# A two-layer attention trunk: attention of one head woven, matmul by matmul, into the projections of the next

## The chip, the cores and the metric

The kernel runs on all eight cores of one Trainium2 chip, one batch element a core, and the cores do not talk to each other. The time is device microseconds of the slowest core, and a lower one is better. A kernel on all cores has two states here. Most executions are fast and agree within 0.3%. In others the cores of one die (0 to 3 or 4 to 7), or of both, show a lower granted clock of TensorE and the run takes some per cent longer.

TensorE is called PE below, as in the profile, with PEld for its weight loads. ScalarE is ACT, VectorE is DVE, GpSimd is POOL, and SP issues most of the transfers.

## The reference

Two layers, x of 2048 rows and 2048 columns on each core. Cut to what matters:

```python
def fox_mixer(h, w_in, b_f, w_out):                 # layer 0: 16 heads of 128
    q, k, v, z, f = split(h @ w_in)
    c = cumsum(log_sigmoid(f + b_f))                # a forget gate for each head
    for i in range(S // Q_BLOCK):                   # causal
        s = q_i @ k.T * scale + c_t - c_s
        s = where(mask, s, -inf)
        outs.append(softmax(s) @ v)
    return (concat(outs) * silu(z)) @ w_out

def diff_mixer(...):                                # layer 1: 8 heads, two 128-wide maps, values 256 wide
    ...
        s = q_i @ k.T * scale + bias                # T5 bias, a constant beyond 128 positions
        p = softmax(where(mask, s, -inf))
        a = p[:, :, 0] - lam * p[:, :, 1]
    ...                                             # RMSNorm of a head, gain
    return (o * silu(z)) @ w_out

for i in range(2):
    x = layer_norm(ALPHA * x + mixer_i(x), ln_g[i], ln_b[i])
```

## The kernel before

Each layer is eight units of 256 columns: two FoX heads, or one differential head. A unit first runs all its projections (q and k at L489, v and z at L517), and only then its attention. A tile of the attention is one block of 128 keys against up to 256 queries: a score matmul, an exponential on ACT, and one or two matmuls with the values. The tile loop keeps these three apart by one tile each.

```python
def do_unit(u, slots):
    proj_fm(sq, qT, r_qT, "act")                    # L489, 512 columns a matmul
    ...
    proj_fm(sk, kT, r_kT, "dve")
    ...
    proj_tm(sv, evac_v)                             # L517, 256 columns
    ...
    proj_tm(sz_slot, evac_z)                        # L547: ACT applies Silu
    ...
    def qk(t):                                      # bank = t % 3
        e.matmul(pb[bank][:, 0:w], lhsT=kT[...], rhs=qT[...], start=True, stop=(len(extra) == 0))
        for n, (k, rhs, _) in enumerate(extra):     # L601: causal mask or T5 bias, added by PE
            e.matmul(pb[bank][:, k * 128:(k + 1) * 128], lhsT=ident[:], rhs=rhs, start=False, ...)
    ...
    for t in range(T + 2):
        if t < T:
            qk(t)
        if 0 <= t - 1 < T:
            ex(t - 1)                               # L618 (FoX) or L623: exponential
        if t - 2 >= 0:
            pv(t - 2)                               # L632: values
```

After the eighth unit come the output projection (L764), the residual and LayerNorm, and the next layer.

The softmax here doesn't subtract the row's maximum and nothing guards it: scores larger than these inputs give would overflow.

Of the kernel before, what the change touches and what calls it, by code (L numbers as in the profile page):

```python
# [16 lines left out]
NB = 16  # L17
KC = 16
# [5 lines left out]
FOX_IN = 8208  # L24
NUM_BUCKETS = 32
MAX_DISTANCE = 128
BIG = 262144.0
EW = 383
# [7 lines left out]

class Prog:
    ENG = ("pe", "act", "dve", "pool", "sp")
# [8 lines left out]
    def _dep(self, op, other):  # L47
        if other is None or other is op:
            return
        if other.dkey is not None:  # L50
            op.waits.append(other)
            return
        if not other.sig:
            lst = self.q[other.eng]
            for k in range(other.idx + 1, len(lst)):
                if lst[k].sig and lst[k].dkey is None and lst[k] is not op:
                    other = lst[k]
                    break
            else:
                other.sig = True  # L60
        op.waits.append(other)

    def _access(self, op, reads, writes):
        for (rg, lo, hi) in reads:
            recs = self.regions.setdefault(rg, [])
            for r in recs:
                if r[0] < hi and lo < r[1]:
                    self._dep(op, r[2])
                    r[3][op.hkey] = op
        for (rg, lo, hi) in writes:  # L70
            recs = self.regions.setdefault(rg, [])
            new = []
            for r in recs:
# [16 lines left out]
    def op(self, eng, fn, reads=(), writes=(), sig=None):  # L90
        o = Op(eng, fn, eng)
        o.idx = len(self.q[eng])
        o.sig = (eng != "pe") if sig is None else sig
        self._access(o, reads, writes)
        self.q[eng].append(o)
        return o
# [20 lines left out]
    def emit(self):  # L117
# [9 lines left out]
        with nc.Block() as block:  # L127
            def mk(ename):
                def body(e):
                    seen = {}  # L130
                    for o in self.q[ename]:
                        for w in o.waits:
# [4 lines left out]
                            if seen.get(k, 0) < v:  # L137
                                e.wait_ge(s, v)  # L138
                                seen[k] = v
# [13 lines left out]

def _t5_bucket(n):
# [7 lines left out]
def _consts():  # L162
    c = np.zeros((128, 3 * 128 + EW), np.float32)
    c[:, 0:128] = np.eye(128, dtype=np.float32)
    c[:, 128:256] = np.triu(np.ones((128, 128), np.float32))
    c[:, 256:384] = 1.0
    for m in range(127, EW):
        c[_t5_bucket(m - 127), 384 + m] += 1.0
        c[31, 384 + m] -= 1.0
    return c  # L170

def build_program(layers):
    nc = bass.Bass("TRN2", target_bir_lowering=False)
    dram_in = lambda n, s: nc.dram_tensor(n, s, F32, kind="ExternalInput").ap()
    x_in = dram_in("x", [S, D])
    xs_in = dram_in("xs", [4, 128, KC * 512])
    consts = dram_in("consts", [128, 3 * 128 + EW])
    ln_g = dram_in("ln_g", [DEPTH, D])
    ln_b = dram_in("ln_b", [DEPTH, D])
    w_in = {}  # L180
    w_out = {}
    if 0 in layers:
        w_in[0] = dram_in("w_in0", [4, 8, 128, KC * 256])
        w_f = dram_in("w_f", [128, KC * 16])
        w_out[0] = dram_in("w_out0", [4, 128, KC * 512])
        b_f = dram_in("b_f", [1, 16])
    if 1 in layers:
        w_in[1] = dram_in("w_in1", [4, 8, 128, KC * 256])
        w_out[1] = dram_in("w_out1", [4, 128, KC * 512])
        lam_q = dram_in("lam_q", [1, 256])  # L190
        lam_k = dram_in("lam_k", [1, 256])
        subln_g = dram_in("subln_g", [1, 256])
        rel_bias = dram_in("rel_bias", [32, 8])
        escr = nc.dram_tensor("escr", [8, 128, EW], F32).ap()
    y_out = nc.dram_tensor("y", [S, D], F32, kind="ExternalOutput").ap()
    x1d = nc.dram_tensor("x1d", [S, D], F32).ap() if len(layers) > 1 else None

    with ExitStack() as st:
        P = Prog(nc, st)
        sb = lambda n, s, d: st.enter_context(nc.sbuf_tensor(n, s, d))  # L200
        XA = sb("XA", [128, 4, KC, 512], BF16)
        XB = sb("XB", [128, 4, KC, 512], BF16)

        def xs(buf, k0, k1, t0, t1):
            st_ = t0 // 512
            lo = t0 - st_ * 512
            hi = t1 - st_ * 512
            if k1 is None:
                return buf[:, st_, k0, lo:hi]
            return buf[:, st_, k0:k1, lo:hi]  # L210
        W = [sb("W%d" % i, [128, KC, 256], BF16) for i in range(3)]
        UW = 18432
        U = sb("U", [128, UW], BF16)
        LW = 7168
        L = sb("L", [128, LW], BF16)
        ident = sb("ident", [128, 128], BF16)
        tri_bf = sb("tri_bf", [128, 128], BF16)
        nmask_bf = sb("nmask_bf", [128, 128], BF16)
        tbt = sb("tbt", [32, 8], F32)
        gtok = [sb("gtok%d" % i, [128, 2, 256], BF16) for i in range(2)]  # L220
        rin = sb("rin", [128, 16], F32)
        lnst = sb("lnst", [128, 32], F32)
        pb = [st.enter_context(nc.psum_tensor("pb%d" % i, [128, 512], F32)) for i in range(8)]

        def rX(buf, kc0, kc1, t0, t1):
            st_ = t0 // 512
            lo, hi = t0 - st_ * 512, t1 - st_ * 512
            if lo == 0 and hi == 512:
                return [(buf, (st_ * KC + kc0) * 1024, (st_ * KC + kc1) * 1024)]
            return [(buf, ((st_ * KC + kc) * 512 + lo) * 2, ((st_ * KC + kc) * 512 + hi) * 2) for kc in range(kc0, kc1)]  # L230
        def rU(lo, hi):
            return [("U", lo * 2, hi * 2)]
        def rL(lo, hi):
            return [("L", lo * 2, hi * 2)]
        def rW(i):
            return [("W%d" % i, 0, KC * 256 * 2)]
        def rPB(i, lo=0, hi=2048):
            return [("pb%d" % i, 0, 2048)]
        def rS(name, lo=0, hi=1 << 20):
            return [(name, lo, hi)]  # L240

        qT = U[:, 0:4096].rearrange("p (m t) -> p m t", m=2)
        kT = U[:, 4096:8192].rearrange("p (m t) -> p m t", m=2)
        V4 = U[:, 8192:12320].rearrange("p (b m c) -> p b m c", b=16, m=2)
        V3 = U[:, 8192:12320].rearrange("p (b c) -> p b c", b=16)
        sz = U[:, 12320:16416].rearrange("p (b c) -> p b c", b=16)
        PT_OFF = 16416
        Pt = [U[:, PT_OFF + s * 256: PT_OFF + (s + 1) * 256] for s in range(4)]
        def r_qT(m, t0, t1): return rU(m * 2048 + t0, m * 2048 + t1)
        def r_kT(m, t0, t1): return rU(4096 + m * 2048 + t0, 4096 + m * 2048 + t1)  # L250
        def r_V(b0, b1): return rU(8192 + b0 * 258, 8192 + b1 * 258)
        def r_sz(b0, b1): return rU(12320 + b0 * 256, 12320 + b1 * 256)
# [28 lines left out]
        def make_layer(li, Xbuf, Xname, Gbuf, Gname, resid_src, resid_reg, out_dst, out_reg, make_next):  # L281
# [218 lines left out]
            def do_unit(u, slots):  # L500
# [223 lines left out]
                for t in range(T + 2):  # L724
                    if t < T:
                        qk(t)
# [224 lines left out]
```

## Time and profile before

| | before |
|---|---|
| time, two fast runs of three | 3348.43 and 3349.73 us (the third, 3596.69, is slow) |
| matmuls, and the sum of their columns | 23,274, 6.905 million |
| the same at N / 2.4 + 2.5 ns each | 2935 us |
| distances between matmul starts beyond that, summed over the trace | 361.4 us |
| ACT table loads | 33 |

The last row but one is worked out from the trace. From the start of each matmul to the start of the next, N / 2.4 + 2.5 ns are taken off, where N is the number of columns; what remains is a gap of PE. With 28 us before the first matmul and 12 after the last the four amounts give some 3336 of 3347.6 us.

The prediction shows the stages. The next lines are the two kinds of unit as a whole, as busy time by stretch (columns: from and to in us, length, then busy us and instruction count of PE, PEld, DVE, ACT and POOL, then granted clock, DMA share and GB/s).

```profile
280.39:453.55 173.16, 164.48 (x1250) 106.08 (x1249) 31.22 (x98) 68.59 (x162) 2.11 (x4) 0.99 0.14 25
1920.07:2097.01 176.94, 171.98 (x1343) 118.84 (x1341) 58.70 (x184) 61.99 (x162) 9.59 (x20) 1.00 0.13 25
```

Over a whole unit ACT has only 68.59 of 173 us, or 61.99 of 177, of work. There is room to hide all of it, if it is spread over the unit and not pressed into the attention.

### The profile page before, as it was taken

How to read it: one execution, taken by the hardware profiler on the slowest of the kernel's cores; microseconds unless marked ns; L12 is line 12 of the kernel's file. 1: busy time of each engine (PE TensorE's matmuls, PEld its weight loads, DVE VectorE, ACT ScalarE, POOL GpSimd, SP SyncE). 2: the span in 40 equal slices, each digit the busy share in tenths (PEclk: the TensorE clock that was granted, in tenths of full speed). 3: DMA queues.
4: the chain of work that ended last, by engine and by line, in shares of the span. 5: the costliest groups of instructions: out<-in, count | busy, mean ns of one | idle time of the engine just before them, and what ended most of it. 6: DMA issues, size and time to landing. Idle time of an engine off the chain costs nothing.

```text
span 3347.6 us, 64426 instructions; the slowest of 8 cores (3340.9 to 3347.6 us)
## 1 busy us (share of the span) xinstructions
PE 3177.2 (95%) x23284; PEld 2027.3 (61%) x23284; DVE 998.7 (30%) x2802; ACT 1173.2 (35%) x2764; POOL 105.5 (3%) x220
## 2 busy tenths in 40 slices
PE   6899898989898999999999999999999999999998
PEld 2747475656566565644457575757676766767443
DVE  0121212121212121246523323242415151514555
ACT  0160707070707061633314233241506060606211
POOL 1000000000000000000000000000000000000000
PEclk9999999999999999999999999999999999999999
DMA  8202020202011110744311010202020202006343
GB/s 141 45 11 39 14 39 14 39 14 38 14 26 26 26 27 14 130 149 146 151 51 27 18 34 14 39 14 39 3 38 14 39 14 39 14 14 102 135 155 139
DMA packets 26754, 171.03 MB, mean 51 GB/s; under 512 B 3376, under 2 KB 7248, under 8 KB 8272
## 3 DMA queue, kind: packets, MB, share of 16 engines
q0 software_dynamic: 12240, 92.41, 15.6%
q1 hardware_dynamic: 14208, 74.51, 6.1%
q8 instruction: 196, 3.21, 0.4%
q14 instruction: 110, 0.90, 0.1%
HBM read 224.19 MB, written 35.12 MB: 77 GB/s over the span
## 4 chain that ended last, share of the span: by engine, by line
PE 85%; ACT 6%; issue 4%; DVE 2%; DMA 2%; ACTq 0%; POOL 0%; DVEq 0%; SPq 0%; POOLq 0%
PE pb L517 27%; PE pb L489 26%; PE pb L764 13%; PE pb L632 12%; ACT U L618 5%; PE pb L598 5%; PE pb L601 2%; DMA XA<-xs 1%; PE pb L644 1%; DMA U<-x 0%; PE pb L807 0%; DVE rin L667 0%; ACTq L138 0%; ACT L618 0%; ACT U L623 0%
## 5 line engine op out<-in xcount | busy, mean ns | idle before, releaser
L632 PE MATMUL pb<-U 128*128 128x129 bf16 (+1 forms) x4352 | 725.1, 247 | 109.0 <-ACT U L618 40.1
L598 PE MATMUL pb<-U 128*128 128x256 bf16 (+1 forms) x2304 | 603.3, 269 | 0.0
L632 PEld LDWEIGHTS pb<-U 128*128 128x128 bf16 x4352 | 323.2, 97 | 399.5 <-issue 332.8
L489 PE MATMUL pb<-XA,W 128*128 128x512 bf16 x2048 | 448.9, 382 | 29.9 <-DMA XA<-xs 29.9
L618 ACT ACTIVATE U<-pb,L 128x256 bf16<-128x256 f32 (+1 forms) x1152 | 451.3, 460 | 24.4 <-PE pb L598 10.6
L517 PE MATMUL pb<-W,XA 128*128 128x256 bf16 x4096 | 450.5, 273 | 0.0
L517 PE MATMUL pb<-W,XB 128*128 128x256 bf16 x4096 | 449.6, 273 | 0.0
L489 PE MATMUL pb<-XB,W 128*128 128x512 bf16 x2048 | 444.6, 379 | 1.3 <-ACT XB L816 1.3
L623 ACT ACTIVATE U<-pb 128x256 bf16<-128x256 f32 (+1 forms) x1152 | 400.4, 372 | 105.6 <-PE pb L598 38.5
L517 PEld LDWEIGHTS pb<-W,XA 128*128 128x128 bf16 x4096 | 401.9, 98 | 49.2 <-issue 0.3
L517 PEld LDWEIGHTS pb<-W,XB 128*128 128x128 bf16 x4096 | 400.5, 98 | 47.9
L489 PEld LDWEIGHTS pb<-XA,W 128*128 128x128 bf16 x2048 | 200.7, 98 | 271.8 <-issue 36.6
L489 PEld LDWEIGHTS pb<-XB,W 128*128 128x128 bf16 x2048 | 199.5, 98 | 239.5 <-issue 1.4
L547 ACT ACT_TABLE_LOAD x16 | 20.5, 1283 | 916.1 <-PE pb L517 916.1
L496 DVE CAST U<-pb 128x512 bf16<-128x512 f32 x128 | 88.6, 692 | 772.2 <-PE pb L489 563.3
L598 PEld LDWEIGHTS pb<-U 128*128 128x128 bf16 x2304 | 224.6, 97 | 11.9
L764 PE MATMUL pb<-XA,XB 128*128 128x512 bf16 x1024 | 225.4, 381 | 2.2 <-DVE U L769 2.2
L764 PE MATMUL pb<-XB,XA 128*128 128x512 bf16 x1024 | 223.0, 381 | 0.0
L494 ACT ACTIVATE U<-pb 128x512 bf16<-128x512 f32 x128 | 76.2, 597 | 394.6 <-PE pb L489 394.6
L540 DVE CAST U<-pb 128x512 bf16<-128x512 f32 x128 | 88.7, 693 | 356.2 <-PE pb L517 356.2
L547 ACT ACTIVATE U<-pb 128x512 bf16<-128x512 f32 x128 | 76.4, 597 | 304.5 <-PE pb L517 304.3
L764 PEld LDWEIGHTS pb<-XA,XB 128*128 128x128 bf16 x1024 | 99.6, 98 | 124.9 <-issue 8.9
(87 smaller groups left out, 1709.5 us busy)
## 6 DMA issues: line engine op xcount, KB each, us to landing
W<-w_in POOLq DMA_DIRECT2D x62, 1024.0 KB, 8.9
U<-x SPq DMA_DIRECT2D x16, 1024.0 KB, 5.0
x1d<-U SPq DMA_DIRECT2D x16, 1024.0 KB, 3.9
U<-x1d SPq DMA_DIRECT2D x16, 1024.0 KB, 4.9
y<-U SPq DMA_DIRECT2D x16, 1024.0 KB, 4.3
XA<-w_out POOLq DMA_DIRECT2D x4, 2048.0 KB, 25.8
XB<-w_out POOLq DMA_DIRECT2D x4, 2048.0 KB, 25.0
XA<-xs POOLq DMA_DIRECT2D x2, 2048.0 KB, 56.5
```

The costliest lines, as they stand in the source:

```text
L489: ins = e.matmul(pb[bk][:, :], lhsT=W[slot][:, kc, m * 128:(m + 1) * 128], rhs=Xbuf[:, tc, kc, :], start=(kc == 0), stop=(kc == KC - 1))
L494: fn = lambda e, m=m, tc=tc, bk=bk: e.activation(out=dstT[:, m, tc * 512:(tc + 1) * 512], in_=pb[bk][:, :], func=AF.Copy)
L496: fn = lambda e, m=m, tc=tc, bk=bk: e.tensor_copy(out=dstT[:, m, tc * 512:(tc + 1) * 512], in_=pb[bk][:, :])
L517: ins = e.matmul(pb[bk][:, bb * 256:(bb + 1) * 256], lhsT=xs(Xbuf, kc, None, b * 128, (b + 1) * 128), rhs=W[slot][:, kc, :], start=(kc == ...
L540: P.op("dve", lambda e: e.tensor_copy(out=dst, in_=src), reads=rPB(bk), writes=r_V(2 * bp, 2 * bp + 2))
L547: P.op("act", lambda e: e.activation(out=sz[:, 2 * bp:2 * bp + 2, :], in_=src, func=AF.Silu), reads=rPB(bk), writes=r_sz(2 * bp, 2 * bp + 2))
L598: ins = e.matmul(pb[bank][:, 0:w], lhsT=kT[:, m, j * 128:(j + 1) * 128], rhs=qT[:, m, q0:q0 + w], start=True, stop=(len(extra) == 0))
L601: ins = e.matmul(pb[bank][:, k * 128:(k + 1) * 128], lhsT=ident[:], rhs=rhs, start=False, stop=(n == len(extra) - 1))
L618: P.op("act", lambda e: e.activation(out=Pt[s][:, 0:w], in_=src, func=AF.Exp, bias=bsel[:, m, j, 2 * I:2 * I + 1], scale=SCALE), reads=rPB ...
L623: P.op("act", lambda e: e.activation(out=Pt[s][:, 0:w], in_=src, func=AF.Exp, scale=SCALE), reads=rPB(bank), writes=rU(PT_OFF + s * 256, P ...
L632: P.op("pe", lambda e, k=k, out=out, rhs=rhs, i=i: e.matmul(out, lhsT=Pt[s][:, k * 128:(k + 1) * 128], rhs=rhs, start=(j == 0), stop=(j == ...
L764: ins = e.matmul(pb[p4][:, :], lhsT=xs(Gbuf, kc, None, b * 128, (b + 1) * 128), rhs=Wo[:, p4, kc, :], start=(kc == 0), stop=(kc == KC - 1))
```

## The change

The change is a rewrite. Its intent is to keep PE on dense projections while ACT computes exponentials, by feeding PE from two lists at once.

1. `merge(F, T)` runs through list F (pieces of 2 to 8 projection matmuls of the next head, or of the output projection) and list T (attention tiles of this head), in proportion to their modelled matmul time.
2. A value matmul follows its score by three FoX or four differential tiles (`LA`) instead of two.
3. The causal mask and the T5 bias leave PE. The exponential is taken without them, and DVE multiplies the result by a 0/1 triangle, or by exp(bias).
4. Silu becomes z (1 + tanh(z/2)), with the factor 2 taken up elsewhere, so that one ACT table serves all.
5. FoX work goes by single heads; forget logits are 16 extra columns of head 0's v and z matmul; LayerNorm goes in pieces of 512 columns; gated outputs of the differential layer are parked in DRAM.
6. PSUM banks are dealt anew: in the differential layer only two banks are left for scores.

```diff
+class Sched:
+    def merge(self, F, T, lead=0.0):
+        ...
+        while f < len(F) or k < len(T):
+            if k < len(T) and (f >= len(F) or cf >= lead + (tf - lead) * ct / tt):
+                ct += T[k][0]
+                self.run(T[k])
+                k += 1
+            else:
+                cf += F[f][0]
+                self.run(F[f])
+                f += 1
...
+LA = (3, 4)
...
-                        for n, (k, rhs, _) in enumerate(extra):
-                            ins = e.matmul(pb[bank][:, k * 128:(k + 1) * 128], lhsT=ident[:], rhs=rhs, start=False, ...)
+                        if j >= 2 * I:
+                            P.op("dve", lambda e: e.tensor_tensor(out=pt.ap[:, 0:128], in0=pt.ap[:, 0:128], in1=tri.ap, op=ALU.mult), ...)
...
-                    P.op("act", lambda e: e.activation(out=sz[...], in_=src, func=AF.Silu), ...)
+            P.op("act", lambda e: e.activation(out=t3, in_=src[:, :, 128:256], func=AF.Tanh, scale=0.5), ...)
+            P.op("dve", lambda e: e.scalar_tensor_tensor(out=F.z3[...], in0=t3, scalar=1.0, in1=src[:, :, 128:256],
+                                                         op0=ALU.add, op1=ALU.mult), ...)
...
+        for u in range(1, NH):
+            F = []                                  # projections of head u
+            ...
+            T = [call(fox_bsel, u - 1)] + fox_att(u - 1, (0, 7, 1, 6, 2, 5, 3, 4))
+            ...
+            sc.merge(F, T, lead=9000 if u == 1 else 0)
```

(The rest of the diff, some 1,800 lines, is buffers, addresses and the same operations in their new places.)

## The prediction

> **What bounds the kernel now.** I read the page first: the busy shares, then the slices over time. The engine that carries the kernel is TensorE (PE), and its share alternates with ScalarE's (ACT).
>
> ```profile
> span 3347.6 us, 64426 instructions; the slowest of 8 cores (3340.9 to 3347.6 us)
> ...
> PE 3177.2 (95%) x23284; PEld 2027.3 (61%) x23284; DVE 998.7 (30%) x2802; ACT 1173.2 (35%) x2764; POOL 105.5 (3%) x220
> ...
> ACT  0160707070707061633314233241506060606211
> PEclk9999999999999999999999999999999999999999
> ```
>
> The ACT row alternates between 6 or 7 and 0 through the first half: in each of the eight units of a layer (256 branch columns: two FoX heads, or one differential head) all the projections run first, ACT idle, then the attention, ACT nearly full. The granted clock never falls below 9. PE's 95% is not a sign of fullness, because ends of matmuls are modelled; so the next view is the chain that ended last, in order of time, for the true lengths of the stages.
>
> ```profile
> 7.52 39.09 DMA XA<-xs
> 46.86 43.29 PE pb L489 x192
> ...
> 104.84 57.92 PE pb L517 x512
> ...
> 280.39 55.91 PE pb L517 x512
> 337.00 1.28 ACT L618
> ...
> 398.11 31.15 PE pb L489 x144
> 429.37 24.17 PE pb L489 x112
> 453.55 55.91 PE pb L517 x512
> ...
> 1920.07 45.41 PE pb L517 x416
> 1965.71 10.49 PE pb L517 x96
> 1977.13 1.07 issue
> 2041.52 31.10 PE pb L489 x144
> ...
> 2097.01 45.41 PE pb L517 x416
> ```
>
> L489 are the q and k projections, 512 columns a matmul: 31.15 us / 144 = 216.3 ns. L517 are v and z, 256 columns: 55.91 / 512 = 109.2 ns. So projections already run dense. A FoX unit takes 453.55 - 280.39 = 173.2 us, of which the attention is 398.11 - (280.39 + 55.91) = 61.8 us. A differential unit takes 2097.01 - 1920.07 = 176.9 us, its attention 2041.52 - (1965.71 + 10.49) = 65.3 us.
>
> What fills these attention stages is seen in the busy times by stretch (columns: length, PE, PEld, DVE, ACT, POOL, then clock, DMA share, GB/s). Projection and attention of a FoX unit come first, then a differential attention:
>
> ```profile
> 281.00:337.00 56.00, 55.72 (x513) 49.77 (x510) 6.74 (x11) 6.06 (x10) 1.16 (x3) 1.00 0.21 39
> 337.00:398.00 61.00, 52.60 (x472) 30.40 (x473) 17.79 (x74) 57.75 (x145) 0.35 (x1) 0.97 0.10 19
> 1977.00:2041.00 64.00, 59.04 (x550) 42.26 (x550) 42.46 (x150) 50.94 (x145) 6.74 (x15) 1.00 0.09 18
> ```
>
> In FoX attention ACT is busy 57.75 of 61 us: the exponentials bound it. In differential attention ACT has 80%, PE waits now and then for an exponential. The groups of instructions give the exponential and the mask and bias matmuls:
>
> ```profile
> L618 ACT ACTIVATE U<-pb,L 128x256 bf16<-128x256 f32 x1024 | 420.4, 472 | 20.5 <-PE pb L598 10.6 <-PE pb L632 2.3 <-ACT U L618 0.4
> L623 ACT ACTIVATE U<-pb 128x256 bf16<-128x256 f32 x1024 | 367.7, 384 | 96.8 <-PE pb L598 37.7 <-PE pb L601 29.5 <-ACT U L623 2.3
> L601 PE MATMUL pb<-L,ident 128*128 128x128 bf16 x992 | 114.0, 219 | 0.0
> L601 PE MATMUL pb<-nmask_bf,ident 128*128 128x128 bf16 x256 | 54.6, 219 | 0.0
> ```
>
> An exponential costs ACT 420.4 / 1024 = 0.41 us (FoX) or 0.36 us (differential), and the same tile costs PE, dense, only 0.11 + 2 x 0.056 = 0.22 us in FoX.
>
> **What the Trainium skill says.** "TensorE: Matmul & The Clock Gate", in "Wait — 56ns, not 53.3ns?", puts back-to-back matmuls of N columns at N / 2.4 GHz + about 2.5 ns. The trace agrees: 216.3 and 109.2 ns above, and sixteen 128-column transposes in a row take 0.89 us, 55.6 ns each, though each loads its own weights: so weight loads hide even under 128 columns. The same page, Part 1, warns of a 13/16 clock once three cores of a die run dense matmuls; this trace disagrees (granted clock 1.00 in the dense stretches, 0.99 over the span, on all eight cores), at least in the fast state. "ScalarE: Activation LUTs", in "Table sets: the hidden batching unit", lists exp and tanh in one set; the kernel before uses Silu between the exponentials and pays 16 table loads for it and 8 + 8 to come back, 1283 ns each in the trace. "Perfetto Trace Analysis", in "Optimization Strategy", advises to interleave regimes with different limiting engines; that is this change.
>
> **The change, part by part.** PE, summed densely. From the built order of instructions the changed kernel has 19,714 matmuls: 8192 of 512 columns, 3840 + 2048 of 256, 256 of 272, 2176 of 257, 2176 of 129, 1024 of 128, two small ones; in all 6.742 million columns. At 2.4 GHz these are 2809 us, plus 19,714 x 2.5 ns = 49 us: 2858 us. The kernel before has 23,274 and 6.905 million columns: 2877 + 58 = 2935 us; its span is 3347.6, so some 410 us are not dense matmul. Where they are, and what happens to each:
>
> 1. FoX attention. Dense, a unit is 128 x 109.2 + 16 x 55.8 (scores) + 272 x 56.3 (values) + 32 x 55.8 (masks) + 32 x 55.8 ns (transposes) = 33.7 us, against 61.8 measured: 28 us wait for ACT, 225 us in eight units. Interleaved, a head (half a unit) spreads its 72 exponentials, 72 x 0.41 = 29 us of ACT, over about 55 us of projections and 16 us of attention on PE; ACT has some 50% and the wait should go. Gain 225 us.
> 2. Differential attention. Dense: 14.9 + 272 x 109.6 ns (values) + 124 x 55.8 (bias) + 32 x 55.8 = 53.4 us against 65.3: 12 us x 8 = 95 us gained likewise (144 exponentials, 52 us of ACT, in a period of some 155 us).
> 3. Mask and bias matmuls leave PE: (256 + 992) x 55.8 ns = 70 us, all of it on the path. In their place come multiplications on DVE (496 of them at most some 0.3 us, an estimate from DVE's 128x128 products, 0.29 us in the trace: below 150 us over an engine that has 70% free), beside other work.
> 4. Start. Before, v and z start at 104.84 us with 256 x 216.3 ns = 55.4 us of matmuls done: 49 us lost. The strips of x arrive one after another, at 160 to 180 GB/s by the busy times between 20 and 75 us. In the changed kernel the same 8 MB and 2.06 MB of weights come first: last strip at about 7 + 10.55 MB / 0.17 = 69 us, and then one strip's work, 14.3 us, plus slack for cold clock: done at about 88 us. By then v, z and the forget logits of head 0 are done as well, 57 us of matmuls; 31 us lost. Gain 18 us. The forget logits become 16 more columns of another matmul (their separate 256 matmuls took 6.9 us, counted in the 49).
> 5. Joints. From the end of the last FoX projection (1375.2) to the end of the output projection (1684.7) are 309.5 us; dense 33.7 + 221 + 14.3 = 269, and 28 of the rest are item 1: 12.6 us lost for the residual's load (it may start only when the attention's tile is free) and for the bias tables' setup. At the second joint 8.4 us. The changed kernel starts the output projection during the last head's attention, but residual tiles again overlay the weights, and the last quarter of w_out is loaded only when the last strip of projections is done: I leave 3 us each. Gain 15 us.
> 6. Tail. 12.2 us from the last matmul to the end; with normalisation in pieces of 512 columns and two half stores, about 10. Gain 2 us.
>
> Sum: 225 + 95 + 70 + 18 + 15 + 2 = 425; 3347.6 - 425 = 2923 us. The other way round: 2858 + 31 + 6 + 10 + 2 (FP32 setup matmuls) = 2907 us. They differ by 16 us because the second assumes no loss inside dense stretches, and the trace has some (the last output projection took 222.8 us for 1024 matmuls, 217.6 ns each instead of 215.8, with clock 0.99). Of 2858 us that is 0.5 to 0.8%. I add 10 us for short waits that the new order makes (bank turns of two projection banks, in-order queues on DVE) and take 2932 us as the time.
>
> **Rivals.** (a) The lookahead is too short: a score matmul may run three FoX tiles ahead, in the differential layer only two score banks remain, and DVE now sits between exponential and value matmul in masked tiles. One tile comes per microsecond, so the slack is 2 us, against about 0.3 (matmul) + 0.4 (ACT) + 0.3 (DVE) plus a 0.7 us DVE evacuation ahead in the queue. It should hold; if each of the 496 multiplied tiles cost PE 0.1 us, 50 us: 2980. (b) Switching between accumulation groups costs time. Against it: in the trace the differential tiles that don't wait run at 0.33 us (values at 2021.47 and 2021.80 us), the dense sum of 109.2 + 2 x 109.6 ns. If each of the 4608 switches cost 10 ns: 46 us more. (c) The power limit: PE dense for 2.8 ms on eight cores trips the limiter. Dense stretches of 227 us ran at 1.00, and one of the three runs before was slow (3596.69). Permanent 13/16 would make 2858 / 0.8125 = 3518 us, slower than before; I give this 3%, and a milder throttle 5%. (d) Weight transfers become late because q, k and v/z each have one buffer. They take 9 us a megabyte (bf16) and are issued one use ahead, some 36 us or more: hidden.
>
> **Range and chances.** Lower end 2890: no losses beyond the second sum, a quicker start. Upper end 3000: rivals (a) and (b) together at half strength, or a clock of 0.97. Only (c) in full could leave the 2% band below 3283 us, so faster 0.96, same 0.02, slower 0.02.
>
> **What would show it.** The ACT row flat at 3 to 5 instead of 7 and 0; three or four table loads instead of 33; a FoX head's period about 72 us and a differential head's about 156 us; 512-column matmuls at about 216 ns wherever no attention lies between; first value of head 0's attention near 98 us; PE starts of the output projection without a wait over 5 us. Waits of value matmuls on ACT or DVE that add to more than 50 us would speak for (a); a clock under 0.97 on undisturbed dies for (c). The prediction is wrong if heads' periods exceed 75 and 162 us, whatever the cause.

## The result, and the profile after

The changed kernel takes 2990.35 us (median of 4 runs, 2988.18 to 2994.85); the kernel before took 3348.24 to 3349.73 in the same rounds (three fast runs; a fourth, slow, took 3596.69). The ratio is 0.8931 (95% interval 0.8914 to 0.8949). Ratios here and below are the mean time of one kernel's fast runs over that of the other's of the same rounds, so not quite the ratio of the medians quoted. So the kernel is faster by 10.7%. The time lies inside the predicted range but 58 us above the predicted point, and most of the experiments ask about those 58.

First the page of the profile after: span, busy shares, and three rows of the slices.

```profile
span 2987.1 us, 59243 instructions; the slowest of 8 cores (2974.2 to 2987.1 us)
...
PE 2887.3 (97%) x19716; PEld 1794.7 (60%) x19716; DVE 1195.9 (40%) x3539; ACT 1242.6 (42%) x3046; POOL 145.1 (5%) x293
...
ACT  0455555555555553453313333434343433442331
PEclk9999999999999999999999999999999999999999
```

The ACT row, which went between 7 and 0, is now flat at 3 to 5, but for the start, the layer switch and the last output projection. The clock is no lower than before (0.992 on this core, 0.992 to 0.995 on all eight).

A FoX head and a differential head, as busy time by stretch:

```profile
237.40:309.20 71.80, 71.80 (x609) 52.78 (x608) 20.25 (x71) 37.38 (x84) 1.58 (x3) 1.00 0.18 31
1907.60:2068.40 160.80, 158.01 (x962) 91.59 (x961) 71.88 (x217) 62.37 (x170) 9.45 (x19) 1.00 0.17 35
```

A FoX head (half a unit of before) takes 71.8 us with PE busy in all of it, where half a unit took 86.6. ACT's share is 37.38 / 71.8, about half. A differential head takes 160.8 where a unit took 176.9, and here 2.8 us of PE are missing.

The groups of instructions answer to the exponential and mask groups that the prediction shows, by form for ACT and DVE (busy us, mean ns, then idle time before them and what ended it):

```profile
L516 ACT ACTIVATE M<-pb,M 128x256 bf16<-128x256 f32 x1024 | 483.4, 473 | 469.0 <-PE pb L528 406.0 <-PE pb L513 27.5 <-DVE M L491 19.9
L808 ACT ACTIVATE M<-pb 128x256 bf16<-128x256 f32 x784 | 299.8, 383 | 483.8 <-PE pb L803 348.9 <-PE pb L823 108.8 <-DVE M L844 9.3
...
L520 DVE TENSOR_TENSOR M<-M 128x128 bf16<-128x128 bf16 x256 | 56.9, 222 | 392.3 <-ACT M L516 391.4 <-issue 0.2
```

The exponentials are as many and as long as before (the differential layer's other 240 are at L814, 383 ns each); what is new is 469 us of idle time in front of the FoX ones. ACT now waits for PE (L528 and L513 are FoX value and score matmuls), not PE for ACT. The mask multiplication costs DVE 0.222 us each, and DVE idles in front of it.

So what does PE still wait for? The waits of PE, summed (line waited at, what released it, then us in total, times, longest):

```profile
PE pb L803 <- DVE M L881: 21.1, 27, 1.3
PE pb L334 <- DMA A<-xs: 20.9, 3, 15.4
PE pb L334 <- DVE M L595: 15.6, 1, 15.6
PE pb L660 <- DVE B L669: 11.0, 2, 9.9
PE pb L334 <- DVE M L841: 8.0, 1, 8.0
```

L334 is every projection, L803 a differential score. The second line is the start, which the prediction counted. The four others are the subject of the experiments. Three of them are single waits of 8 to 16 us and one is a series of 27 small ones.

The gaps between matmul starts, worked out as in the table of before, now sum to 98.9 us (361.4 before). Split by stretch, they stand against the terms of the prediction like this:

| term | predicted, us | after, us |
|---|---|---|
| matmuls dense | 2858 | 2858 |
| start: time before the first matmul, and gaps up to 100 us | 31 | 15.4 + 17.5 = 32.9 |
| 100 to 1100 us: FoX heads | | 4.9 |
| 1100 to 1300 us: joint 1, output projection of the FoX layer | 3 (the joint) | 20.5 |
| 1300 to 1500 us: layer switch | 0 | 12.9 |
| 1500 to 2600 us: differential heads | | 25.2 |
| 2600 to 2800 us: joint 2 | 3 (the joint) | 16.4 |
| the rest, up to the last matmul | | 1.4 |
| FP32 matmuls, losses inside dense stretches, short waits | 2 + 15 + 10 | (in the rows above) |
| tail | 10 | 12.4 |
| sum | 2932 | 2984.7 of 2987.1 |

The remaining 2.4 us lie in what the sum doesn't model, such as the last matmul's own length. FoX heads lost 4.9 us in 1000, the 0.5% that the prediction expected of dense stretches. The excess sits in four places. The table is of core 0, the slowest. The differential heads lost 25.3 to 25.4 us on each of the six cores whose record is whole, but the joints vary: the longest gap is 7.5 to 15.8 us at joint 1 over the eight cores (median 12.3), 6.9 to 11.1 at the layer switch (8.8) and 7.0 to 12.4 at joint 2 (8.8). So the wait of a single core there is good to a few us only.

**Joint 1.** The timeline where the output projection starts (start, us, engine, line, operation, count, then idle time before it and its releaser):

```profile
1178.07 1.89 PE L334 MATMUL pb<-A,B 128*128 128x512 bf16 x8
...
1194.72 0.69 DVE L595 SCALAR_TENSOR_TENSOR M<-M,pb 128x512 f32<-128x512 f32 x1 [20.58 <-DMA M<-x]
...
1195.56 5.56 PE L334 MATMUL pb<-A,B 128*128 128x512 bf16 x16 [15.60 <-DVE M L595]
```

PE has filled both projection banks and waits for DVE to read one, and DVE waits for the first residual tile. The transfers issued in these 45 us (columns: KB each, median us from issue to landing):

```profile
M<-x SPq DMA_DIRECT2D x3, 1024.0 KB, 25.7
A<-w0o POOLq DMA_DIRECT2D x1, 2048.0 KB, 23.3
```

Three residual tiles and the last quarter of w_out are under way together, and a residual tile takes 25.7 us to land. The median of all sixteen residual tiles is 5.1 us here and 5.0 in the kernel before, though at its own joint that kernel waited for a tile too, 14.5 us of its critical chain.

After the wait sixteen matmuls take 5.56 us, 0.35 us each, where 0.216 is usual; the first eight start 0.43 us apart. This is the half clock that the Trainium skill describes in "TensorE: Matmul & The Clock Gate", "What's actually happening": 1.2 GHz after about 3.4 us of idling. The trace agrees on the speed: the clock granted from 1195.5 to 1199.4 us is 0.50, 0.98 after it, and 512 columns take 0.427 us for about 3.4 us, 1.7 us lost at this wait. How long PE must idle for it isn't shown here.

**Layer switch.** The same view where the normalised rows are transposed for the next layer:

```profile
1394.77 1.89 PE L334 MATMUL pb<-A,B 128*128 128x512 bf16 x8
...
1401.55 0.42 DVE L720 TENSOR_TENSOR M<-M 128x256 f32<-128x256 f32 x1 [9.68 <-DMA M<-lam_k]
1405.65 0.69 DVE L669 COPY B<-pb 128x1024 bf16<-128x1024 bf16 x1
1406.58 1.01 PE L660 MATMUL pb<-M 128*128 128x128 bf16 x8 [9.92 <-DVE B L669]
```

PE's transposes (L660) need the bank that DVE empties with the copy L669. Ahead of that copy in DVE's queue stands the first instruction of the lambda setup, L720, which waits 9.68 us for a small transfer. The copy has its data and stands behind it, and behind the rest of the setup and some of the normalisation, 4.1 us more.

**Differential heads.** One of the 27 short waits:

```profile
1669.77 0.39 PE L876 MATMUL pb<-M 128*128 128x128 bf16 x4
...
1670.22 0.42 DVE L776 CAST M<-pb 128x256 bf16<-128x256 f32 x1
1670.76 0.43 DVE L778 TENSOR_TENSOR A<-M 128x256 bf16<-128x256 f32 x1
1671.10 0.42 DVE L816 TENSOR_TENSOR M<-M 128x256 bf16<-128x256 f32 x1
1671.44 0.42 DVE L881 COPY M<-pb 128x512 bf16<-128x512 bf16 x1
...
1672.00 0.27 PE L803 MATMUL pb<-A 128*128 128x256 bf16 x1 [0.71 <-DVE M L881]
```

The transposes L876 land in one of the two score banks. DVE copies them out at L881 only after three instructions that are no part of this. A score matmul that comes to the same bank two turns later waits.

### The profile page after: what moved, and what is told of

Same layout as the page of the kernel before. It is cut to its first block, busy times and chain, and to the rows that moved or that the text cites. A ratio compares the mean times of both kernels' runs of the same rounds, so it can differ in the third digit from the quotient of the medians.

```text
span 2987.1 us, 59243 instructions; the slowest of 8 cores (2974.2 to 2987.1 us)
## 1 busy us (share of the span) xinstructions
PE 2887.3 (97%) x19716; PEld 1794.7 (60%) x19716; DVE 1195.9 (40%) x3539; ACT 1242.6 (42%) x3046; POOL 145.1 (5%) x293
## 4 chain that ended last, share of the span: by engine, by line
PE 93%; DMA 3%; DVE 2%; issue 1%; ACT 0%; POOL 0%; DVEq 0%; SPq 0%; ACTq 0%; POOLq 0%
PE pb L334 71%; PE pb L823 8%; PE pb L528 4%; PE pb L803 4%; PE pb L513 4%; DMA A<-xs 1%; DMA M<-x 1%; DMA M<-lam_k 1%; DMA M<-x1d 1%; PE pb L555 1%; PE pb L660 0%; DVE M L881 0%; PE pb L876 0%; DVE M L856 0%; DVE M L636 0%
## 5 line engine op out<-in xcount | busy, mean ns | idle before, releaser
L516 ACT ACTIVATE M<-pb,M 128x256 bf16<-128x256 f32 (+1 forms) x1152 | 524.8, 461 | 506.8 <-PE pb L528 439.7
L334 PE MATMUL pb<-A,M 128*128 128x512 bf16 x2048 | 535.2, 382 | 22.1 <-DMA A<-xs 20.9
L334 PE MATMUL pb<-M,A 128*128 128x256 bf16 (+1 forms) x4096 | 543.2, 274 | 4.9 <-DMA M<-w0vzf 4.9
L334 PE MATMUL pb<-M,B 128*128 128x512 bf16 x2048 | 526.9, 379 | 0.0
L334 PE MATMUL pb<-B,M 128*128 128x512 bf16 x2048 | 524.7, 379 | 0.0
L808 ACT ACTIVATE M<-pb 128x256 bf16<-128x256 f32 x784 | 299.8, 383 | 483.8 <-PE pb L803 348.9
L334 PEld LDWEIGHTS pb<-M,A 128*128 128x128 bf16 x4096 | 378.3, 98 | 44.0 <-issue 5.8
L803 PE MATMUL pb<-A 128*128 128x256 bf16 (+1 forms) x1152 | 307.1, 267 | 23.1 <-DVE M L881 21.1
L528 PE MATMUL pb<-M 128*128 128x129 bf16 x2176 | 310.8, 220 | 0.5 <-DVE M L520 0.3
L513 PE MATMUL pb<-M 128*128 128x256 bf16 (+1 forms) x1152 | 306.2, 267 | 0.5 <-DVE M L469 0.4
L334 PEld LDWEIGHTS pb<-B,M 128*128 128x128 bf16 x2048 | 199.7, 98 | 134.5
L334 PEld LDWEIGHTS pb<-M,B 128*128 128x128 bf16 x2048 | 200.0, 98 | 131.9
L334 PEld LDWEIGHTS pb<-A,M 128*128 128x128 bf16 x2048 | 179.1, 98 | 139.8 <-issue 28.4
L334 PE MATMUL pb<-A,B 128*128 128x512 bf16 x1024 | 240.7, 383 | 15.6 <-DVE M L595 15.6
L528 PEld LDWEIGHTS pb<-M 128*128 128x128 bf16 x2176 | 206.3, 98 | 81.8 <-issue 4.6
L334 PE MATMUL pb<-B,A 128*128 128x512 bf16 x1024 | 242.6, 381 | 8.0 <-DVE M L841 8.0
L816 DVE TENSOR_TENSOR M<-M 128x256 bf16<-128x256 f32 (+1 forms) x368 | 135.2, 375 | 283.2 <-ACT M L814 249.4
L814 ACT ACTIVATE M<-pb 128x256 f32<-128x256 f32 (+1 forms) x368 | 126.6, 346 | 223.4 <-PE pb L803 171.3
L520 DVE TENSOR_TENSOR M<-M 128x128 bf16<-128x128 bf16 x256 | 56.9, 222 | 392.3 <-ACT M L516 391.4
L823 PE MATMUL pb<-M 128*128 128x257 bf16 x1088 | 213.6, 274 | 0.2
L823 PE MATMUL pb<-A,M 128*128 128x257 bf16 x1088 | 213.5, 274 | 0.0
L803 PEld LDWEIGHTS pb<-A 128*128 128x128 bf16 x1152 | 112.7, 98 | 165.1 <-issue 40.2
## 6 DMA issues: line engine op xcount, KB each, us to landing
M<-w1vz POOLq DMA_DIRECT2D x8, 2048.0 KB, 13.9
```

Of the source, the lines that this page charges most:

```text
L334: ins = e.matmul(out, lhsT=lhs(kc), rhs=rhs(kc), start=(kc == 0), stop=(kc == KC - 1))
L513: P.op("pe", lambda e: e.matmul(pb[s][:, 0:w], lhsT=F.k.ap[:, j * 128:(j + 1) * 128], rhs=F.q.ap[:, i0 * 128:i0 * 128 + w], start=True, st ...
L516: P.op("act", lambda e: e.activation(out=pt.ap[:, 0:w], in_=pb[s][:, 0:w], func=AF.Exp, bias=bs.ap[:, j * 8 + I:j * 8 + I + 1], scale=SCAL ...
L520: P.op("dve", lambda e: e.tensor_tensor(out=pt.ap[:, 0:128], in0=pt.ap[:, 0:128], in1=tri.ap, op=ALU.mult), reads=pt.rr(0, 128) + tri.r, w ...
L528: P.op("pe", lambda e, n=n, k=k, first=first: e.matmul(pb[b][:, k * 129:(k + 1) * 129], lhsT=pt.ap[:, n * 128:(n + 1) * 128], rhs=F.v3[:, ...
L803: P.op("pe", lambda e: e.matmul(pb[s][:, 0:w], lhsT=Dv.k3[:, m, j * 128:(j + 1) * 128], rhs=Dv.q3[:, m, i0 * 128:i0 * 128 + w], start=True ...
```

## The experiments

Each kernel ran beside the kernel before on the same chip. Three chips served; the medians of the kernel before's fast runs on them are 3347.7 to 3349.4 us, so a difference quoted in us carries up to 2 us of this. The edits are against the changed kernel, unless it says otherwise.

### Is it really the hidden ACT time?

The first two kernels took the interleave away and left everything else: the list of projections first, then the list of tiles. `e1_fox_in_turn` did it for the FoX heads 0 to 13.

```diff
-            sc.merge(F, T, lead=9000 if u == 1 else 0)
+            if u < NH - 1:
+                sc.merge(F, [])
+                sc.merge([], T)
+            else:
+                sc.merge(F, T)
```

> FoX heads 0 to 13 run after the next head's projections instead of between them; all else as in the changed kernel (2990 us). If the gain of the FoX layer is ScalarE's time hidden under projections, each head's attention alone takes its exponentials, 64 x 0.41 + 8 x 0.36 = 29 us, instead of 16 us of dense matmuls: 13 to 15 us a head, 14 heads, 180 to 210 us: about 3170 to 3200 us. If the gain came from the mask matmuls and the longer lookahead (three tiles, three score banks), running in turn costs under 60 us.

Its result was wrong (relative error 0.029). The last three value matmuls of a head are pending when its tiles are over. In this order they ran after the next head's projections had overwritten values that they read. The times were 3179.84 us in a fast run and 3227.69 in a slow one, with the right amount of work in nearly the right order, but a wrong kernel proves little.

`e2_diff_in_turn` did the same for the differential heads 0 to 5.

```diff
-            sc.merge(F, T)
+                sc.merge(F, T)
+            else:
+                sc.merge(F, [])
+                sc.merge([], T)
```

> The same for differential heads 0 to 5. If the 12 us a unit of the kernel before are waits for exponentials and masks that only interleaving hides: + 12 x 6 = 72 us, about 3060 us. If what cost time there was mainly the bias matmuls (now gone), the attention alone is 50.5 us of exponentials against 46.5 us of matmuls: + 4 x 6 = 24 us, about 3015 us.

It was wrong for the same reason (0.050), and all four runs were slow (3293.98 to 3484.83 us). Nothing is concluded from it.

Both were mended by emptying the list of pending value matmuls after each head: `e1b_fox_in_turn` and `e2b_diff_in_turn`.

```diff
-                sc.merge([], T)
+                sc.merge([], T + [call(drain)])
```

> e1 again with the pending value matmuls of a head emitted before the next projections overwrite its values (e1 left them behind and was wrong). Theory as for e1: 13 to 15 us a head, 3170 to 3200 us; rival: under 3050 us.

The result was correct, but all five runs fell into the slow state (3387.39 to 3542.2 us). So the cores of the undisturbed die of the profiled run have to do: 3174.6 to 3190.5 us at a clock of 0.988 to 0.991, against die medians of 2982.9 and 2980.3 in the changed kernel. One head on core 1, by stretch:

```profile
405.60:491.70 86.10, 81.19 (x608) 53.97 (x608) 20.83 (x71) 32.26 (x84) 1.58 (x3) 1.00 0.15 26
```

and the ACT timeline of a head's attention on the same core:

```profile
406.01 9.38 ACT L516 ACTIVATE M<-pb,M 128x256 bf16<-128x256 f32 x25 [1.24 <-DVE M L491]
416.14 17.51 ACT L516 ACTIVATE M<-pb,M 128x256 bf16<-128x256 f32 x47 [0.74 <-PE pb L513]
```

All 72 exponentials of a head run back to back, 0.37 us apart, in 27.6 us, with hardly a break: ACT bounds the attention again. The head takes 86.1 us instead of 71.8, and 14 x 14.3 = 200 us is about what these cores lost (3178.6, the median of the die, less 2982 is 197). The interleave of the FoX layer is worth 14.3 us a head, 28.6 us a unit.

> e2 again, mended likewise. e2's undisturbed die needed some 3155 to 3167 us, far over both expectations (3060, 3015). New theory: with two score banks a score matmul must wait until the exponential two tiles back has left its bank, so matmul, semaphore and exponential no longer overlap fully and a tile costs about 0.5 us: 144 tiles x 0.5 = 72 us against 46.5 dense: 26 us a head, 6 heads: 3145 to 3165 us. If the old figure of 12 us holds, 3060 us.

Correct, 3160.26 us (3158.08 to 3160.55), ratio 0.9417 (0.9356 to 0.9479): 170 us slower than the changed kernel, 28.3 us for each of six heads. A head on core 0, by stretch:

```profile
1889.30:2078.50 189.20, 173.80 (x961) 84.93 (x960) 72.02 (x215) 61.94 (x170) 9.70 (x19) 0.99 0.14 30
```

28 us a head is more than twice the 12 us a unit that the kernel before lost, and it makes the head longer (189) than a unit was (177). Split by which matmul comes next, 21 of the 28 us are gaps before a score matmul. The changed kernel has only two score banks in this layer, where the kernel before had three. On this core, 80 of the 144 scores, with 20 us of gaps, start within 0.15 us of the end of an exponential, and ACT is not full:

```profile
2049.90 0.71 ACT L808 ACTIVATE M<-pb 128x256 bf16<-128x256 f32 x2 [0.33 <-PE pb L803]
2050.85 0.71 ACT L808 ACTIVATE M<-pb 128x256 bf16<-128x256 f32 x2 [0.23 <-PE pb L803]
```

Two exponentials, 0.71 us, come every 0.95 us. That fits waits for one of the two banks. A version in turn with a third bank was not run, so the number of banks as the cause is argued and not shown. What is shown is that the differential layer in this arrangement, without the interleave, is slower than the old one.

The next kernel tested rival (a) of the prediction from its other end. `e9_ahead_1` shortens the distance from score to value.

```diff
-LA = (3, 4)
+LA = (1, 1)
```

> Value matmuls follow one tile behind the score matmuls instead of three (FoX) and four (differential). Theory of the prediction: matmul, semaphore and exponential take 0.8 to 0.9 us, a masked tile 1.1 to 1.3 us, a tile comes per 1.0 us: unmasked tiles just fit, but gates and copies on ACT and masks don't: + 60 to + 200 us, 3050 to 3190 us. If the lookahead didn't matter once projections lie between: within 15 us of 2990.

Correct, 3235.18 us (3233.81 to 3236.55), ratio 0.9664 (0.9643 to 0.9685). It is slower than the range expected: the cost was underrated. A FoX head takes 80.1 us and a differential one 176.8. The waits of PE (core 7):

```profile
PE pb L823 <- DVE M L816: 102.2, 133, 2.6
PE pb L528 <- DVE M L520: 51.4, 89, 1.7
...
PE pb L528 <- ACT M L516: 3.0, 10, 0.5
```

Value matmuls (L823, L528) wait above all for DVE's multiplication (L816, L520), which the change put between exponential and value. In the changed kernel the same wait is 0.3 us in all. One tile of lookahead is about one microsecond (72 tiles in a FoX head of 71.8 us), and a chain of score, exponential and multiplication with its queues does not fit into it. With three or four it fits. So two thirds of the gain of this change are lost with a lookahead of one: 3235.18 - 2990.35 = 245 us of 359. The kernel before had two tiles; two were not run in the new order.

`e8_silu` puts Silu back in place of tanh (in the differential layer likewise).

```diff
-            P.op("act", lambda e: e.activation(out=t3, in_=src[:, :, 128:256], func=AF.Tanh, scale=0.5), ...)
-            P.op("dve", lambda e: e.scalar_tensor_tensor(out=F.z3[...], in0=t3, scalar=1.0, in1=src[...], op0=ALU.add, op1=ALU.mult), ...)
+            P.op("act", lambda e: e.activation(out=F.z3[...], in_=src[:, :, 128:256], func=AF.Silu), ...)
```

> Silu in place of tanh for the gate, in the interleaved order; VectorE's product for it goes. Theory: Silu and exp lie in different table sets, each of 264 gates costs two loads of 1283 ns and holds up the exponentials by about 3 us, longer than the two to three tiles of slack: PE waits 1 to 2 us each time: 3250 to 3450 us, some 528 loads. Rival (the lookahead of three and four tiles swallows it): under 3010 us.

Correct, 3290.18 us (3288.26 and 3292.1), ratio 0.9828 (0.9807 to 0.9849), within the range expected. Five sixths of the gain are lost, 300 of 359 us, and what is left is under 2%. The ACT timeline shows why (core 4):

```profile
402.02 1.57 ACT L514 ACTIVATE M<-pb,M 128x256 bf16<-128x256 f32 x4
403.98 1.28 ACT L423 ACT_TABLE_LOAD   x1 [0.39 <-PE pb L334]
405.27 0.38 ACT L423 ACTIVATE M<-pb 128x256 bf16<-128x256 f32 x1
405.67 1.28 ACT L514 ACT_TABLE_LOAD   x1
406.97 1.57 ACT L514 ACTIVATE M<-pb,M 128x256 bf16<-128x256 f32 x4
```

Silu (L423) and the exponentials (L514) need different tables, and in the interleaved order they alternate. Each Silu stops the exponentials for two loads and itself (403.98 to 406.97, 3.0 us), about three tiles' worth. PE's waits show what runs out:

```profile
PE pb L511 <- ACT M L514: 81.9, 115, 2.3
PE pb L799 <- ACT M L804: 75.5, 60, 2.3
PE pb L799 <- ACT M L810: 64.5, 35, 2.2
```

It is score matmuls (L511, L799) that wait for exponentials, 222 us, and not value matmuls: the score banks, three and two, run out before the lookahead does. There are 468 loads where the changed kernel has 3. So the tanh form, which looks like a detail, is a condition of the interleave.

### The masks on DVE

`e7_mask_on_pe` gives the FoX causal mask back to PE, by the identity matmul of the kernel before, and removes DVE's multiplication.

```diff
-                        P.op("pe", lambda e: e.matmul(pb[s][:, 0:w], ..., start=True, stop=True), ...)
+                        def score(e):
+                            ins = e.matmul(pb[s][:, 0:w], ..., start=True, stop=(j < 2 * I))
+                            if j >= 2 * I:
+                                ins = e.matmul(pb[s][:, 0:128], lhsT=ident.ap, rhs=nmask.ap, start=False, stop=True)
+                            return ins
...
-                        if j >= 2 * I:
-                            P.op("dve", lambda e: e.tensor_tensor(out=pt.ap[:, 0:128], in0=pt.ap[:, 0:128], in1=tri.ap, op=ALU.mult), ...)
```

> In the FoX layer the causal mask goes back to PE as 256 matmuls of 128 columns added into the score bank, and VectorE's 256 multiplications go. If PE is the bound to the nanosecond, + 256 x 55.8 ns = 14.3 us: 3004 us. If the multiplications on VectorE cost PE waits of their own (rival of the prediction, 0.1 us each on 256), the difference is under 0: 2990 us or less.

Correct. Of four runs one is slow (3324.53 us), and one that counts as fast has two cores at a clock of 0.982 and 0.983 (3027.25). With it the ratio is 0.8971 (0.889 to 0.9052), too wide for a difference of some ten us. The two undisturbed runs took 3001.17 and 3000.89 us, 11 above 2990.35. The period of a FoX head settles it: 72.53 us on all eight cores where the changed kernel has 71.82, so 0.71 us a head, 11.4 in sixteen, where 16 x 55.8 ns = 0.89 us a head, 14.3 in all, of matmuls came back. The rest is gaps that went with the multiplications: the FoX heads lose 1.7 us instead of 4.9. So matmuls removed from PE here were worth four fifths of their dense time. The 992 bias matmuls of the differential layer were not tested alone.

### Where the 58 us are

**Score banks.** `e3_tr_bank` lets the differential transposes use a projection bank: a transpose is held back until a group of projection matmuls is at its middle, when the other projection bank has been emptied, and goes there.

```diff
+                    if k0 == KC // 2 and pj["tr"]:
+                        pj["tr"].popleft()(1 - b)
...
-            def tr():
-                s = s_bank()
+            def tr(s):
...
-            sc.after(8000, tr)
+            sc.after(8000, lambda: pj["tr"].append(tr))
```

> The transposes of a finished differential pair write the idle one of the two projection banks, half way through a projection group, instead of one of the two score banks. Theory: the 28 us of excess before score matmuls in the differential layer (27 waits of 0.6 to 1.6 us on the copy out of the transposes) are turned off: 2962 to 2966 us, and the waits of score matmuls on that copy vanish. Rival (score matmuls wait for exponentials in two banks anyway): under 8 us gained, the waits move to ACT.

Correct, 2972.52 us (2972.3 to 2972.81), ratio 0.8875 (0.8857 to 0.8892): 18 us gained, less than the 24 to 28 expected. The waits of PE (core 3; the extra lines of the edit move L595 to L597 and L841 to L843):

```profile
PE pb L334 <- DVE M L843: 17.9, 1, 17.9
PE pb L334 <- DVE M L597: 14.2, 1, 14.2
PE pb L662 <- DVE B L671: 12.7, 2, 11.6
```

The 27 waits are gone. In gaps between matmul starts, 1500 to 2600 us went from 25.2 to 1.8 us, so the score banks cost 23 us. But 2600 to 2800 us went from 16.4 to 24.9: the wait at joint 2 grew from 8.0 to 17.9 (over the eight cores the longest gap there went from 7.0 to 12.4 up to 14.6 to 18.0). PE arrives 26 us earlier on these cores, and the first residual tile is issued 27 us earlier, but it takes 27.4 us to land instead of 16.0 (23.0 to 27.4 over the cores, against 14.8 to 20.2). Why that transfer is slower was not looked into; that e5, which loads the tile earlier, removes the wait agrees with it. On the cores shown, a third of what was removed in one place came back in another.

**The layer switch.** `e4_setup_late` puts the lambda setup off, so that its transfer has landed when DVE comes to it.

```diff
-            sc.after(8000, lambda: diff_setup2(lq, lk))
+            sc.after(30000, lambda: diff_setup2(lq, lk))
...
-            sc.after(20000, ex)
+            sc.after(34000 if u == 0 else 20000, ex)
```

> The setup of the differential layer's scalars is emitted 22 us later in the model's time, so that VectorE doesn't stand at it until the lambda vectors have landed. Theory: VectorE's in-order queue blocks the copy of the transposes of x1, PE waits 10.1 us and then runs 1.7 us slower at half clock: 2978 to 2981 us. Rival (VectorE is simply late with normalisation there): no change, within 2 us.

Correct, 2980.31 us (2978.0 to 2982.26), ratio 0.8897 (0.8882 to 0.8913): 10 us gained. The waits of PE (core 2):

```profile
...
PE pb L334 <- DVE M L841: 12.4, 1, 12.4
...
PE pb L660 <- DVE B L669: 1.1, 1, 1.1
```

The wait at L660 went from 11.0 to 1.1 us, with nothing moved but the setup's place in the queues; the longest gap there is 0.5 us on all eight cores. That confirms that the copy stood behind the setup and was not slow itself. "Perfetto Trace Analysis" of the Trainium skill says in "Tensor Engine Instruction (MATMUL, LD_WEIGHTS)" that DVE works its queue strictly first in, first out. The trace agrees: DVE stood at L720 for 9.68 us with the 0.69 us copy behind it, and PE waited 9.92.

**The joints.** `e5_res_early` puts the first residual tile into the one of the three buffers that overlays no weights, and issues its load a head earlier.

```diff
-            x = xres[li][b % 3]
+            x = xres[li][(b + 2) % 3]
...
+                F.append(call(load_res, 0, 0))
...
-        load_res(0, 0)
```

(The index in three places; the same two lines for layer 1.)

> The first residual tile of each output projection goes to the buffer that is free all along and is loaded one head earlier. Theory: PE's waits of 15.8 and 8.2 us at the two joints are waits for the residual tile, which shares the DMA queues with the last quarter of w_out; with the first tile early the second tile (landing 23 us after the joint, wanted at about 17) becomes the wait: about 5 us left at each joint: 2970 to 2976 us. Rival: the last quarter of w_out lands so late that it sets the time: 2985 us or more.

Correct, but this chip was unruly: two fast runs (2975.14 and 2973.01 us), four slow ones (3191.57 to 3493.57). From the fast runs, 16 us gained. The waits of PE in one of them (core 4):

```profile
PE pb L660 <- DVE B L669: 14.8, 2, 13.7
PE pb L334 <- DVE M L595: 5.6, 1, 5.6
...
```

Joint 1's wait went from 15.6 to 5.6 us, and the wait of 8.0 at joint 2 left the list. Over the eight cores the longest gap is now 4.2 to 5.8 us at joint 1 and at most 2.4 at joint 2. The layer switch may have taken some of it back: its wait is 14.8 here against 11.0, but over the cores the longest gap there went from 6.9 to 11.1 up to 8.7 to 13.9, so the ranges overlap.

**All three.** `e6_three` is the sum of the three edits.

> e3, e4 and e5 together. If the waits they take away are independent: 2990 - 26 (transposes) - 12 (setup) - 10 and - 8 (residual tiles) = 2934 us. Alone, e3 gave only 18 us, because the wait at the second joint grew from 8 to 16 us; with e5's early tile there it should not. If the second joint is really set by the last quarter of w_out, part comes back: up to 2945 us.

Correct, three fast runs of 2941.35 to 2942.42 us (median 2941.39) and a slow one (2996.97), ratio 0.8787 (0.8771 to 0.8803). This is the best version, 1.6% better than the changed kernel. It gains 49 us, and the three alone gained 18 + 10 + 16 = 44. Joint 2 still gives something back: the longest gap there, at most 2.4 us in e5, is 5.3 to 7.0 us on the eight cores. The waits of PE that are left (core 0):

```profile
PE pb L334 <- DMA A<-xs: 23.4, 3, 18.1
PE pb L876 <- DVE M L597: 5.9, 1, 5.9
PE pb L334 <- DVE M L597: 4.9, 1, 4.9
```

These are the start, joint 2 and joint 1. `e10_three_late_third` asked what still holds joint 1: the third residual tile, whose load runs beside the last quarter of w_out, or that quarter itself. It is e6 with that load put off.

```diff
-        load_res(0, 2)
+        sc.after(12000, lambda: load_res(0, 2))
...
-        load_res(1, 2)
+        sc.after(12000, lambda: load_res(1, 2))
```

> e6 with the load of the third residual tile at each joint put off by some 12 us, so that the second tile shares the DMA queues with the last quarter of w_out alone. Theory: what is left of the wait at the first joint (5.8 us in e5) is that second tile: 3 to 5 us under e6. If it is the last quarter of w_out, the same as e6 within 2 us.

Correct, the fast runs between 2940.63 and 2941.86 us, two slow; ratio 0.8786 (0.8768 to 0.8805). It is the same as e6, so the third tile is not what holds joint 1. The wait there (core 2):

```profile
PE pb L334 <- DMA A<-w0o: 5.5, 1, 5.5
```

All eight cores wait for w_out here, 3.6 to 5.5 us; in e6 five of them already did. What sets joint 1 now is the last quarter of w_out, which is written over x's last strip and so may only start once the last projection has read it.

## Why the prediction was right, and where it was wrong

**What was right.** Item 1, FoX attention, 28 us a unit: the interleave is worth 14.3 us a head by e1b, 28.6 a unit, and the head's period is 71.8 us (about 72 predicted). Here the reason is confirmed and not just the size, since in e1b the 72 exponentials stand back to back again.

Item 2, differential attention: the period is 160.8 us, above the 156 predicted and inside the limit of 162 given. The 12 us a unit describe the kernel before. In the new arrangement the interleave itself carries 28 (e2b), probably because it also pays for a lost score bank. The prediction named the two banks only as a rival and didn't see that double role. With the waits for score banks gone (e6) the period is 157.3 us.

Item 3, masks: e7 gave 11 us for FoX, where the item's rate makes 14.3. The multiplications take 0.222 us each on 128x128 and 0.422 on 128x256 with FP32 (L816), against "at most some 0.3 us"; they are 624 (256 + 368), not 496, and take 56.9 + 135.2 = 192 us, not "below 150 us". In the FoX layer they cost PE some 3 us of gaps (e7). Item 4, the start: 32.9 us lost, 31 predicted. Item 6, the tail: 12.4 us, 10 predicted; it has not become shorter than the 12.2 of before, so these 2 us of gain did not come.

**Rivals.** (a) did not come true: PE's wait for masked FoX tiles is 0.3 us in all. But e9 shows that the margin was needed: with one tile of lookahead the price is 245 us. (b) did not either: from a value matmul to a projection matmul the starts show about 1 ns beyond N / 2.4 + 2.5. (c) the fast runs of the changed kernel show a clock of 0.988 to 0.995. (d) in the list of waits weights appear only for head 0, at the start (4.9 and 1.2 us). Two of the signs failed: the first value of head 0's attention came at 103.9 us and not near 98, and the output projection began with a wait of 15.6 us and not under 5.

**What was wrong.** Three steps, which make 50 of the 55 us between the predicted time and the profiled span.

1. Item 5: "I leave 3 us each". Mis-sized. The single waits were 15.6 and 8.0 us, and 20.5 and 16.4 us of gaps lie in those stretches. The item named both of the causes, that "residual tiles again overlay the weights" and that "the last quarter of w_out is loaded only when the last strip of projections is done", and did not work out that the two share the DMA engines at that moment. A residual tile took 25.7 us (median of the three), where 5.0 is the median of the kernel before. An estimate was to be had from the trace of before: three tiles of 1 MB and 2 MB of w_out are 5.24 MB, and at the 160 to 180 GB/s of its start they take about 30 us, far more than the three left. Loading the first tile earlier removed 10 of the 15.6 (e5; 7 by the medians of the cores), and what is left is the quarter of w_out (e10).
2. "I add 10 us for short waits". Mis-sized: the waits for score banks alone cost 23 us, the amount that e3 took away between 1500 and 2600 us. The sentence names "bank turns of two projection banks, in-order queues on DVE". The bank turns that mattered were those of the score banks, which the transposes share with the scores.
3. The layer switch was left at zero. It cost 12.9 us: a queue on DVE that works in order, with an instruction at its head that waits for a transfer (e4), and then the half clock. "In-order queues on DVE" was named, as part of those 10 us; that one such instruction can stop PE for 10 us at once was not.

The three corrections make 2932 + (36.9 - 6) + (31.5 - 25) + 12.9 = 2982 us, where 31.5 are the gaps of the FoX and differential heads and of the rest, against the 25 allowed for dense losses and short waits. With the start's 2 and the tail's 2.4 it is 2987, the span of the profile. And the kernel without those three faults (e6) takes 2941.4 us, 9 above the predicted point.

**What stays open.** The bias part of item 3 was not isolated. Whether the two score banks are the cause of e2b's 28 us, and where between one and three tiles the lookahead becomes too short, was not tested.

## What to carry to other kernels

When two stages lean on different engines, weave them instruction by instruction. But first take out what cannot be woven, such as functions of two ACT tables, and give the chain between the engines more than one tile of lookahead: each of the two faults alone took back 245 to 300 of the 359 us here. Then look for single waits of 8 to 16 us at the joints between stages, where an instruction waits for a transfer at the head of an in-order queue or two transfers are wanted in the same moment. A gain that you get ahead of such a joint is partly given back there until the joint itself is mended.

## What the Trainium skill lacked or had wrong

- "TensorE: Matmul & The Clock Gate", "Back-to-back issue gap", gives some 81 ns for 128 columns and 131 ns for 512 as what a long stream of weight load and matmul sustains, and calls N / 2.4 + 2.5 an isolated gap. Here that formula holds in long streams, each matmul with its own weights: 55.6 ns for 128 columns (sixteen in a row), 216.3 ns for 512 (144 in a row), and 4.9 us in 1000 us of mixed widths beyond it.
- The same page, Part 1, expects a 13/16 clock once three cores of a die run dense matmuls. With eight cores dense for 2.9 ms, the fast runs of the changed kernel show 0.988 to 0.995 on all of them. Slow runs of a variant show 0.82 to 0.94 on one die or both (e5, two fast runs of six). The page has no word on a state that comes and goes from run to run.
- "ScalarE: Activation LUTs", "What ACT_TABLE_LOAD costs", puts a switch at 2.66 us, 1.28 for the load and 1.38 for a drain. The load is right, 1283 ns. No drain shows in e8: a load begins 0.02 us after the Silu before it ends, and both loads with the Silu between take 3.0 us.
- No page says what an instruction that waits for a transfer costs the engines behind an in-order queue; "Perfetto Trace Analysis" only states the order. Here it was 9.7 us on DVE and 9.9 us on PE.
- "Perfetto Trace Analysis", "Optimization Strategy", says that interleaving regimes may help, without a size or conditions. Here the ratio is 0.8931 and, with the joints mended, 0.8787; with two ACT tables 0.9828, with one tile of lookahead 0.9664.
